# A diffusion backbone's first stage rebuilt: four latent projections per feature tile, context keys and values by group

## The chip, the core and the metric

The kernel runs on one core of one Trainium2 chip. The time is device microseconds of that core for one execution; it stands as the median of three runs. Five engines take part: TensorE (PE; its weight loads are listed as PEld), VectorE (DVE), ScalarE (ACT), GpSimd (POOL) and SyncE (SP, which issues most transfers).

## The reference

Two layers run over 1024 latent tokens of width 1024, with 256 context tokens beside them. The first is windowed attention (16 query heads in four groups, head width 128), the second a convolution module. Shift, scale and gate of each layer come from a linear map of a condition vector.

```python
shift, scale, gate = split(silu(c) @ ada_w[i] + ada_b[i], 3)        # 1024 -> 3 x 1024
h_lat = rmsnorm(x, norm_g[i]) * (1 + scale) + shift                 # latent tokens
h_ctx = the same of ctx with silu(c_ctx)                            # layer 0 only
# layer 0
q, k, v, z = h_lat @ w_in       # 2048, 512, 512, 2048 columns; q and k rotated by position
kc, vc     = h_ctx @ w_in[:, k and v columns]
o = softmax([sink, q kc, q k (|i-j| <= 128)] / sqrt(128)) @ [vc, v]
x = x + gate * ((o * silu(z)) @ w_out)
# layer 1
a, gl, z = h_lat @ w_in + b_in
u = layernorm(depthwise_conv31(a * sigmoid(gl)) + b)
x = x + gate * ((silu(u) * silu(z)) @ w_out)
return rmsnorm(x, final_g)
```

All inputs and outputs are fp32.

## The kernel before

**Arithmetic.** A matmul with full precision is done as three matmuls of type fp32r: each operand is split into a high half (a copy on ACT, L147) and a low half (a subtraction of the high half on DVE or POOL, `split_lo`, L156), and `mm3` (L194) multiplies high by high, high by low and low by high. So each operand costs an ACT copy and a DVE or POOL subtraction before PE can use it. Activations are kept turned: feature on the partition, token along the row. A *feature tile* is 128 of the 1024 features (eight tiles, `kt`), a *pair* (`pr`) two of them, a *half* 512 of the 1024 tokens.

**Places.** SBUF is handed out in 45 pages of 4 KB per partition (`pg`, names that end in `_page`) and 6 smaller ones (`hp`, `_half`). PSUM has two tiles of two banks (`ps_s`, shown as pss), two single banks o0 and o1 (`ps_o`, pso) and a pair of banks (`ps_g`, psg). Weights of the attention layer come in 512 KB chunks of 128 columns (`WStream`, L199: `load` issues the transfer on SP's queue, `split` makes the halves, `need` does both if they are late, `done` frees).

**Order.** Every engine call goes through the class `InOrder` (L77), which is why each row of the trace has line 87. A scheduler orders the instructions of an engine by its own estimate, unless `pin` (L104) puts the engine into program order. Before, nothing is pinned in the first stage, and PE alone from line 999 on.

**First stage (L303 to L463 and L987 to L998).** For each of four pairs: the modulation vector of the pair's 256 features is computed by 512-column matmuls over the condition vector (8 of plain fp32 for each of pairs 0 and 3, 16 of fp32r with split weights for each of 1 and 2; L384 to L399), its row is copied out of PSUM and turned into columns by four small matmuls (L403 to L413). Then the pair's two context tiles are modulated and split, and the keys and values of the context of all four groups are accumulated in the two pss tiles, 8 x 3 matmuls of 256 columns per tile (L421 to L436; weights from `kv_load`, L290). Then the pair's two latent tiles of the first half are modulated and split, and two projections are accumulated: keys of group 0 and queries of head 0 (`kq`, L447 to L458). Rows of the context and the first half are normalised and turned ahead of that (`normalise`, L326; `turned`, L335), those of the second half after the last pair's matmuls are issued. After the loop the second half is modulated (`mod_x1`), keys and queries are rotated (`rope`, L805, which swaps halves by two transfers on ACT's queue), context keys and values are split (`ctx_out`, L488), and three more half projections run alone (L995 to L998).

**Attention (L1000 to L1052).** 16 heads by 8 query blocks of 128 give 128 steps. A step issues the scores of the next block (`scores`, L900; the softmax behind them runs on DVE, ACT and POOL), then 12 matmuls of a later projection as fill (`fill`, L887, from the queue `fillq`: the gate z and the query of the coming heads, each 48 matmuls), then the product with the values for a half of a head (`pv`, L956), then the transposes of the block's softmax (`transposes`, L935). Where the next head opens a group (`regroup`, L1024), the group's keys and values are projected at that place. Background work runs in small pieces: `ada_rest` (the remaining modulation vectors, on DVE) and `low_parts` (low halves of the output weights).

**Then** comes the attention's output projection (`proj_attn`, L627) in four quarters of half by 512 columns, each with four blocks of 128 tokens in PSUM banks listed at L694; its first matmuls are already used as fill in the last head (`early_proj`, from block `EARLY_FROM`). In the last quarter the last three weight pieces are held back and each block is finished by itself, followed by its evacuation (`evac0`, L728). The conv stage and the kernel's output projection follow, the latter with the same scheme of quarters and a bank list of its own.

## Time and profile before

| | |
|---|---|
| median of three runs | 1807.83 us (1807.12 to 1808.11) |
| profiled execution, time and span | 1810.63 us, 1808.8 us |
| mean granted TensorE clock | 0.986 |
| busy share PE, PEld | 96%, 79% |
| busy share DVE, ACT, POOL | 69%, 49%, 45% |
| moved by DMA | 246.66 MB, mean 136 GB/s |

The share of busy time is an average over stages. Rows of the trace read: start in us, duration in us, engine, line, operation, output tile and inputs, shape and type, then in brackets how long the engine stood idle before it and what released it. Matmuls are pipelined, so their durations overlap, and PE's rate is read from the distance of their starts. A row of the view by stretches gives the stretch, its length, the busy time and count of PE, PEld, DVE, ACT and POOL in this order, the granted TensorE clock as a share of full speed, the busy share of the DMA engines and the GB/s that they moved. Tile names are the program's without their numbers: `araw`, `ahi`, `alo` are the modulation weights and their halves, `wraw`, `whi`, `wlo` the projection weights', `kvh` and `kvl` the context weights', `fc` and `fx` modulated context and latent tiles before they are split into `hch`, `hcl` and `hh`, `hl`; `x_page` holds token rows.

### The profile page before, as it was taken

To read this page: it belongs to the slowest core of one execution; us is meant where nothing else is said; L and a number is where in the kernel's file an instruction comes from. 1 tells how busy PE (TensorE), PEld (TensorE's weight loads), DVE (VectorE), ACT (ScalarE), POOL (GpSimd) and SP (SyncE) were. 2 spreads that over 40 slices of the span, in tenths; PEclk is the share of its full clock that TensorE was granted. 3 is DMA by queue.
4 is the path that set the end of the run, shared out by engine and by line. 5 is a ranking of instruction groups with operands and counts; after the bars stand their busy time and mean duration, and the time that the engine had idled before them with its cause. 6 is when DMAs were issued, how large, how long until landed. Compare 5 with 4: busy or idle time off the path is not lost. (4 is left out here: it accounts for less than half of the span.)

```text
span 1808.8 us, 23987 instructions
## 1 busy us (share of the span) xinstructions
PE 1740.4 (96%) x8383; PEld 1425.1 (79%) x8383; DVE 1253.6 (69%) x2429; ACT 883.3 (49%) x1535; POOL 812.9 (45%) x624
## 2 busy tenths in 40 slices
PE   6889999999999999999999989999999999999997
PEld 3577888888778887888788877888888888788886
DVE  5566677577657875675614349999999999866733
ACT  4444444445444554444533426655556565366630
POOL 1553334233433344342200137999888788220300
PEclk8999999999999999999999999999999999999999
DMA  9422344244334444333877723111020202376881
GB/s 339 136 63 82 114 152 143 90 136 143 117 105 128 149 135 130 91 120 120 302 279 244 261 76 104 48 35 47 24 88 30 82 30 70 113 247 227 316 290 47
DMA packets 196478, 246.66 MB, mean 136 GB/s; under 512 B 11926, under 2 KB 126918, under 8 KB 196356
## 3 DMA queue, kind: packets, MB, share of 16 engines
q1 hardware_dynamic: 189668, 234.29, 39.2%
q10 hardware_dynamic: 6688, 10.83, 2.4%
q8 instruction: 66, 1.08, 0.2%
q14 instruction: 56, 0.46, 0.1%
HBM read 192.90 MB, written 41.69 MB: 130 GB/s over the span
## 5 line engine op out<-in xcount | busy, mean ns | idle before, releaser
L87 POOL TENSOR_TENSOR odd_half<-odd_half,prod_half 128x513 f32<-128x513 f32 (+2 forms) x252 | 318.0, 1269 | 20.9 <-ACT prod_half L87 7.4
L87 PE MATMUL psg<-hh_page,whi_page 128*128 128x512 f32 x632 | 253.6, 401 | 3.1 <-DVE rope_half L87 3.1
L87 PE MATMUL psg<-hh_page,wlo_page 128*128 128x512 f32 x632 | 251.4, 398 | 0.0
L87 PE MATMUL psg<-hl_page,whi_page 128*128 128x512 f32 x632 | 251.3, 398 | 0.0
L87 POOL TENSOR_TENSOR wlo_page<-wraw_page,whi_page 128x1024 fp32r<-128x1024 f32 x72 | 174.9, 2431 | 139.8 <-ACT whi_page L87 87.6
L87 POOL TENSOR_SCALAR p_page<-p_page,sc 128x640 f32<-128x640 f32 (+1 forms) x128 | 104.8, 819 | 284.5 <-DVE sc L87 149.0
L87 ACT ACTIVATE prod_half<-ubuf,dww 128x513 f32<-128x513 f32 (+2 forms) x252 | 165.2, 674 | 110.2 <-POOL odd_half L87 106.2
L87 ACT ACTIVATE p_page<-p_page,sc 128x640 f32<-128x640 f32 (+1 forms) x128 | 102.6, 801 | 170.2 <-DVE sc L87 162.2
L87 PE MATMUL psg<-h2l_page,whi_page 128*128 128x512 f32 x456 | 179.6, 394 | 1.8 <-DVE h2l_page L87 1.8
L87 PE MATMUL psg<-h2h_page,whi_page 128*128 128x512 f32 x456 | 181.1, 397 | 0.0
L87 PE MATMUL psg<-h2h_page,wlo_page 128*128 128x512 f32 x456 | 179.7, 394 | 0.0
L87 DVE SCALAR_TENSOR_TENSOR pss<-ubuf,wsum,pss 128x512 f32<-128x512 f32 (+3 forms) x270 | 172.7, 674 | 0.3
L87 DVE SCALAR_TENSOR_TENSOR pss<-ubuf,dww,pss 128x512 f32<-128x512 f32 (+3 forms) x270 | 172.5, 674 | 0.3
L87 PEld LDWEIGHTS psg<-hh_page,wlo_page 128*128 128x128 f32 x632 | 120.1, 190 | 28.2
L87 PEld LDWEIGHTS psg<-hh_page,whi_page 128*128 128x128 f32 x632 | 120.7, 191 | 26.3 <-DVE rope_half L87 3.5
L87 PEld LDWEIGHTS psg<-hl_page,whi_page 128*128 128x128 f32 x632 | 120.5, 191 | 22.4
L87 PE MATMUL pso<-h2l_page,whi_page 128*128 128x512 f32 x312 | 122.9, 394 | 0.0
L87 PE MATMUL pso<-h2h_page,whi_page 128*128 128x512 f32 x312 | 122.9, 394 | 0.0
L87 PE MATMUL pso<-h2h_page,wlo_page 128*128 128x512 f32 x312 | 122.6, 393 | 0.0
L87 ACT ACTIVATE whi_page<-wraw_page 128x1024 fp32r<-128x1024 f32 x88 | 92.8, 1054 | 60.9 <-PE psg L87 20.4
L87 DVE TENSOR_TENSOR ptlo<-pss,pthi 128x640 fp32r<-128x640 f32 (+1 forms) x144 | 103.0, 715 | 25.9 <-ACT pthi L87 25.7
L87 ACT ACTIVATE pthi<-pss 128x640 fp32r<-128x640 f32 (+1 forms) x144 | 88.3, 613 | 65.0 <-PE pss L87 48.5
(247 smaller groups left out, 4080.9 us busy)
## 6 DMA issues: line engine op xcount, KB each, us to landing
wraw_page<-in_conv_w_in_dram SPq DMA_DIRECT2D x48, 512.0 KB, 3.9
wraw_page<-in_attn_w_in_dram SPq DMA_DIRECT2D x40, 512.0 KB, 4.7
wo_page<-in_attn_w_out_dram SPq DMA_DIRECT2D x32, 512.0 KB, 4.3
wol_page<-wolA SPq DMA_DIRECT2D x32, 512.0 KB, 7.5
wo_page<-in_conv_w_out_dram SPq DMA_DIRECT2D x32, 512.0 KB, 8.1
wol_page<-wolC SPq DMA_DIRECT2D x32, 512.0 KB, 7.0
rope_half<-rope_half ACTq DMA_DIRECT2D x80, 128.0 KB, 2.4
araw_page<-in_ada_w_dram SPq DMA_DIRECT2D x32, 256.0 KB, 4.6
```

The costliest lines, as they stand in the source:

```text
L87: r = f(*a, **k)
```

## The change

- **Loads.** The first half's latent rows come first, then three pairs of modulation weights with two weight chunks behind each of the first two, then the context rows. The separate 4 MB load of key and value weights is gone.
- **Modulation.** All but one 256-row piece is split and multiplied as fp32r. The functions `ada_split`, `ada_mm` and `ada_cols` are called a pair ahead of the tiles that use them.
- **First half.** For each feature tile, four projections of the latent tokens (key, query, value, gate of head 0) run instead of two, into the four banks of the pss tiles. Latent tiles are modulated straight out of the transposes' bank. PE and DVE are pinned to program order.
- **Context.** Context tiles are turned, modulated and split as cover between the latent ones. Keys and values of the context are projected for group 0 only, and for the other groups in their own jobs (a third part, `half == 2`); the tiles `hch` and `hcl` stay until the last group's values are done.
- **Second half.** Four projections per tile again, each tile modulated two tiles ahead; the first scores are issued after its sixth tile's matmuls. The remaining outputs are emptied in the order value, key, query, gate.
- **Attention.** 18 matmuls of the next head's query run before the loop; then the query of a coming head stands ahead of its gate in the queue. The early part of the output projection starts at the last head's first block, at 10 matmuls a step. A weight chunk is split after 15 matmuls of a job's second part instead of at the end of its first. At a change of group the gate that is left in the queue is issued first. One of the two extra steps of `ada_rest` moves from block 3 to block 1.
- **Last quarters.** The bank lists of the two last quarters alternate the pss tiles: (2, 3, 0, 1) becomes (2, 0, 3, 1) in the attention projection, (5, 0, 1, 2) becomes (0, 5, 1, 2) in the kernel's last. Banks 0 and 1 are the halves of one pss tile, 2 and 3 of the other.

```diff
+SPLIT_AT = 14
+ADA_FP = ((0, 0),)
+LAST_FILL = 10
 FILL = 12
 DEFER = 6
 EARLY = 2
 EARLY_ROWS = 6
-EARLY_FROM = 4
+EARLY_FROM = 0
...
-    add_chunk(("q", 0), wcol(0))
-    add_chunk(("v", 0), wv[0])
-    add_chunk(("k", 0), wk[0])
-    for g in range(NG):
-        for h in range(4 * g, 4 * g + 4):
-            add_chunk(("z", h), wcol(AW + 2 * KW + h * P))
-            if h + 1 < NH:
-                add_chunk(("q", h + 1), wcol((h + 1) * P))
-        if g + 1 < NG:
-            add_chunk(("k", g + 1), wk[g + 1])
-            add_chunk(("v", g + 1), wv[g + 1])
-    wsA = WStream(chunks, lo_eng=lambda i: V if i in (1, 2) else G)
+    for key, src in (("k", 0), wk[0]), (("q", 0), wcol(0)), (("v", 0), wv[0]), (("z", 0), wcol(AW + 2 * KW)):
+        add_chunk(key, src)
+    for h in range(NH - 1):
+        add_chunk(("q", h + 1), wcol((h + 1) * P))
+        add_chunk(("z", h + 1), wcol(AW + 2 * KW + (h + 1) * P))
+        if h % 4 == 3:
+            add_chunk(("k", h // 4 + 1), wk[h // 4 + 1])
+            add_chunk(("v", h // 4 + 1), wv[h // 4 + 1])
+    wsA = WStream(chunks, nraw=4, lo_eng=lambda i: V if i in (2, 4) else G)
...
-    def kv_load(pr):
-        kvraw[pr] = [pg.alloc(F32, [1024], "kvraw") for _ in range(2)]
-        for i in range(2):
-            kt = 2 * pr + i
-            SY.dma_start(out=kvraw[pr][i], in_=W[kt * P:kt * P + P, AW:AW + 2 * KW])
...
+    xs0 = load_rows(x[0, 0:512], 4)
     ada_load(0)
+    wsA.load()
+    wsA.load()
+    ada_load(1)
+    wsA.load()
+    wsA.load()
+    ada_load(2)
     cx = load_rows(ctx[0], 2)
-    kv_load(0)
-    xs0 = load_rows(x[0, 0:512], 4)
-    wsA.load()
...
-    ck = [ps_s(), ps_s()]
-    kq = None
-    wq = None
-    def mod_x1(kt):
-        h, l = Hh[kt][:, 512:1024], Hl[kt][:, 512:1024]
-        modulate(fx1[kt], fx1[kt], kt, 0)
-        act(h, fx1[kt], AF.Copy)
-        split_lo(G if kt % 2 else V, l, fx1[kt], h)
-        if kt % 2:
-            pg.free(fx1_pg[kt // 2])
-    for pr in range(NPR):
...
-            for j in range(8):
-                c = ck[j // 4][:, j % 4 * CT:j % 4 * CT + CT]
-                mm3(c, wh[:, j], wl[:, j], h, l, kt == 0 and j % 2 == 0, kt == KT - 1 and j % 2 == 1)
...
-            mm3(kq[0], wh[:, 0], wl[:, 0], h, l, kt == 0, kt == KT - 1)
-            mm3(kq[1], wq[0][:, kt], wq[1][:, kt], h, l, kt == 0, kt == KT - 1)
...
+    def ada_split(pr):
+        for i in range(4):
+            if (pr, i) not in ADA_FP:
+                raw = araw[pr][i]
+                rv = raw.rearrange("p a b c -> p a (b c)")
+                h, l = pg.alloc(F32R, [2, 512], "ahi"), pg.alloc(F32R, [2, 512], "alo")
+                act(h, rv, AF.Copy)
+                split_lo(V, l, rv, h)
+                pg.free(raw)
+                araw[pr][i] = (h, l)
+    def ada_mm(pr):
+        o = ps_o(0)
+        for i in range(4):
+            for k in range(2):
+                if (pr, i) in ADA_FP:
+                    r = araw[pr][i].rearrange("p a b c -> p a (b c)")
+                    parts = [(cf, r)]
+                else:
+                    parts = [(c4, r) for r in araw[pr][i]]
+                for n, (c, r) in enumerate(parts):
+                    PE.matmul(o[0:4], c[:, 2 * i + k, :], r[:, k], start=i + k + n == 0,
+                              stop=i + k == 4 and n == len(parts) - 1)
+            pg.free(*(araw[pr][i] if len(parts) == 2 else (araw[pr][i],)))
+        V.tensor_copy(R[pr][0:4, 0:512], o[0:4])
+    def ada_cols(pr):
+        rw, m = R.pop(pr), mods[pr]
+        cps = ps_o(1)
+        for i in range(4):
+            PE.matmul(cps[:, 2 * i:2 * i + 2], rw[0:5, i * P:(i + 1) * P], sel[0:5], start=True, stop=True)
+        hp.free(rw)
+        with tc.high_priority():
+            V.tensor_copy(m[:, 0:2], cps[:, 0:4].rearrange("p (a b) -> p a b", b=2))
+            for i in range(2):
+                V.tensor_scalar(out=m[:, 2 + i], in0=cps[:, 4 + 2 * i:6 + 2 * i], scalar1=1.0,
+                                scalar2=vt[:, 96 + 2 * pr + i:97 + 2 * pr + i], op0=ALU.add, op1=ALU.mult)
+    def turn(ts, kt, bank):
+        tp = bank()
+        for i in range(len(ts)):
+            PE.transpose(tp[:, i * P:(i + 1) * P], ts[i][:, kt * P:(kt + 1) * P], ident)
+        return tp
+    def x_tile(tp, kt, half, eng):
+        if half == 0:
+            Hh.append(pg.alloc(F32R, [1024], "hh"))
+            Hl.append(pg.alloc(F32R, [1024], "hl"))
+        sl = slice(half * 512, half * 512 + 512)
+        m, i = mods[kt // 2], kt % 2
+        with tc.high_priority():
+            modulated(tp, [(Hh[kt][:, sl], Hl[kt][:, sl], lambda f: f[:, 0:512])], m[:, 2 + i, 0:1], m[:, i, 0:1], 512, eng)
+    def c_tile(kt, bank=1):
+        m, i = mods[kt // 2], kt % 2
+        if kt % 4 == 0:
+            Hc.append((pg.alloc(F32R, [4, CT], "hch"), pg.alloc(F32R, [4, CT], "hcl")))
+        h, l = (t[:, kt % 4] for t in Hc[kt // 4])
+        modulated(turn(cx, kt, lambda: ps_o(bank))[:, 0:CT], [(h, l, lambda f: f[:, 0:CT])],
+                  m[:, 2 + i, 1:2], m[:, i, 1:2], CT, V)
+        if kt == KT - 1:
+            pg.free(*cx)
+    def x_mm(kt, half, acc, which):
+        sl = slice(half * 512, half * 512 + 512)
+        for n in which:
+            w = wsA.hl[n]
+            mm3(acc[n], w[0][:, kt], w[1][:, kt], Hh[kt][:, sl], Hl[kt][:, sl], kt == 0, kt == KT - 1)
...
+    pin("PV")
+    normalise(xs0, (V, V, G, G))
+    ada_split(0)
+    ada_mm(0)
+    ada_load(3)
+    ada_cols(0)
+    for _ in range(2):
+        wsA.split()
+    tps = [turn(xs0, kt, ps_g) for kt in range(2)]
+    sa, sb = ps_s(), ps_s()
+    acc0 = [t[:, i * 512:i * 512 + 512] for t in (sa, sb) for i in range(2)]
+    ctodo = deque(range(KT))
+    x_tile(tps[0], 0, 0, V)
+    x_tile(tps[1], 1, 0, V)
+    x_mm(0, 0, acc0, (0, 1))
+    x_mm(1, 0, acc0, (0, 1))
+    ada_split(1)
+    for _ in range(2):
+        wsA.split()
+    for pr in range(NPR):
+        a, b = 2 * pr, 2 * pr + 1
+        which = range(4) if pr else (2, 3)
+        if pr + 1 < NPR:
+            ada_mm(pr + 1)
+        if pr == 1:
+            normalise(cx, (G, G))
+        if pr == NPR - 1:
+            normalise(xs1, (G, G, G, G))
+        if pr + 2 < NPR:
+            ada_split(pr + 2)
+        x_mm(a, 0, acc0, which)
+        if pr + 1 < NPR:
+            tp = turn(xs0, a + 2, ps_g)
+            ada_cols(pr + 1)
+            x_tile(tp, a + 2, 0, V)
+        if pr > 1:
+            c_tile(ctodo.popleft())
+        x_mm(b, 0, acc0, which)
+        if pr + 1 < NPR:
+            x_tile(turn(xs0, b + 2, ps_g), b + 2, 0, G)
+        if pr > 0:
+            c_tile(ctodo.popleft())
+        if pr == 1:
+            xs1 = load_rows(x[0, 512:1024], 4)
...
-            acc = [banks[b] for b in ((4, 5, 0, 1), (2, 3, 4, 5), (0, 1, 4, 5), (2, 3, 0, 1))[s]]
+            acc = [banks[b] for b in ((4, 5, 0, 1), (2, 3, 4, 5), (0, 1, 4, 5), (2, 0, 3, 1))[s]]
...
+        if kind in "kv" and half == 2:
+            c = kvt[n][2]
+            if kind == "k":
+                act(c[:, 0], o[:, 0:CT], AF.Copy)
+                split_lo(V, c[:, 1], o[:, 0:CT], c[:, 0])
+                return None
...
+    def gemm_ctx(wc, o):
+        for kt in range(KT):
+            h, l = (t[:, kt % 4] for t in Hc[kt // 4])
+            for a, b in ((0, h), (0, l), (1, h)):
+                PE.matmul(o[:, 0:CT], wc[a][:, kt], b, start=kt == 0 and a == 0 and b is h, stop=kt == KT - 1 and a == 1)
+                yield
+    PARTS = {"q": (0, 1), "z": (0, 1), "k": (0, 1, 2), "v": (2, 0, 1)}
...
+            for m, _ in enumerate(gh):
+                yield
+                if m == DEFER - 1 and late:
+                    late()
+                if m == SPLIT_AT and half == PARTS[kind][1] and wsA.ns <= i + 1:
+                    wsA.split()
+                    wsA.load()
...
-            kc = (kch, kcl)[b]
             PE.matmul(s[:, w0:512], q[a][:, qsl], kk[b][:, ksl], start=n == 0, stop=n == 2)
-            PE.matmul(s[:, 512:768], q[a][:, qsl], kc[:, g], start=n == 0, stop=n == 2)
+            PE.matmul(s[:, 512:768], q[a][:, qsl], c[:, b], start=n == 0, stop=n == 2)
...
+    pin("P")
+    tps = []
+    while ctodo:
+        c_tile(ctodo.popleft(), len(ctodo) % 2)
+        if len(tps) < 2:
+            tps.append(turn(xs1, len(tps), ps_g))
+    d0 = [target(kind, 0) for kind in "kqvz"]
+    tails = []
+    def finished0(half, acc, which=range(4)):
+        for n in which:
+            t = finish("kqvz"[n], 0, half, acc[n], d0[n])
+            if t:
+                tails.append(t)
+    finished0(0, acc0)
+    for kind, n in (("k", 0), ("v", 2)):
+        o = ps_g()
+        for _ in gemm_ctx(wsA.hl[n], o):
+            pass
+        t = finish(kind, 0, 2, o, d0[n])
+        if t:
+            tails.append(t)
+        x_tile(tps.pop(0), n // 2, 1, V)
...
+    sa = ps_s()
+    acc1 = [sa[:, 0:512], sa[:, 512:1024], ps_g(), ps_g()]
     for kt in range(KT):
-        mod_x1(kt)
-    rope(kq[0], h0, *(t[:, h0] for t in kvt[0]))
-    rope(kq[1], h0, *(t[:, h0] for t in qt[0]))
-    ctx_out()
-    run(job(("v", 0), (0,)))
+        x_mm(kt, 1, acc1, range(4))
+        if kt + 2 < KT:
+            x_tile(turn(xs1, kt + 2, lambda: ps_o(kt % 2)), kt + 2, 1, G if kt % 2 else V)
+        if kt >= 2 and tails:
+            tails.pop(0)()
+        if kt == 0:
+            wsA.load()
+        if kt == 5:
+            pg.free(*xs1)
+            wsA.split()
+            scores(0, 0)
+    for i in range(4):
+        wsA.done(i)
+    wsA.nraw = 2
+    wsA.load()
+    finished0(1, acc1, (2, 0, 1, 3))
...
-    run(job(("k", 0), (1,)))
-    run(job(("q", 0), (1,)))
-    pin("P")
...
-    scores(0, 0)
     pvq = deque()
-    enqueue(("z", 0))
     enqueue(("q", 1))
-    run(job(("v", 0), (1,)))
+    fill(18)
+    tails.pop()()
     for _ in range(2):
         next(adag)
     for i, (h, qb) in enumerate(steps):
         if qb == 0:
             if h + 1 < NH:
+                if h:
+                    enqueue(("q", h + 1))
                 enqueue(("z", h + 1))
-            if h + 2 < NH:
-                enqueue(("q", h + 2))
...
-        if lstate[0] == "open" or h and (h % 4 < 3 or qb < LOWS):
+        if lstate[0] == "open" or 0 < h < NH - 1 and (h % 4 < 3 or qb < LOWS):
...
-            fill(FILL)
+            fill(FILL if h < NH - 1 else LAST_FILL)
...
+            fill(1000, ("z", h + 1))
             run(job(("k", g)))
...
-        for _ in range(2 if qb == 3 or qb == 6 and h % 2 else 1):
+        for _ in range(2 if qb == 1 or qb == 6 and h % 2 else 1):
...
-            acc = [banks[b] for b in ((0, 1, 2, 3), (4, 5, 0, 1), (2, 3, 6, 4), (5, 0, 1, 2))[s]]
+            acc = [banks[b] for b in ((0, 1, 2, 3), (4, 5, 0, 1), (2, 3, 6, 4), (0, 5, 1, 2))[s]]
```

More of the change, by code (lines that the diff above doesn't have):

```diff
@@ L823, in job @@
         wc = wsA.need(i)
[L824 to L839 removed]
+        d = target(kind, n)
```

234 lines of the change are left out of this document (54 added, 180 removed).

## The prediction

> **What bounds the kernel now.** I read the page first, then the busy time in stretches of 20 us, then PE's waits in order of time, then the other engines' instructions around those waits.
>
> ```profile
> PE 1740.4 (96%) x8383; PEld 1425.1 (79%) x8383; DVE 1253.6 (69%) x2429; ACT 883.3 (49%) x1535; POOL 812.9 (45%) x624
> ```
> ```profile
> 0.00:20.00 20.00, 10.26 (x25) 2.50 (x25) 3.40 (x15) 7.31 (x11) 1.63 (x8) 1.00 0.83 292
> 20.00:40.00 20.00, 14.73 (x76) 11.14 (x76) 17.07 (x28) 10.73 (x20) 6.10 (x3) 0.70 1.08 374
> 40.00:60.00 20.00, 14.84 (x71) 8.81 (x69) 14.90 (x21) 10.98 (x16) 10.43 (x5) 0.84 0.89 301
> 60.00:80.00 20.00, 20.00 (x98) 11.41 (x97) 8.07 (x17) 9.19 (x16) 5.91 (x3) 0.95 0.34 106
> 80.00:100.00 20.00, 18.09 (x121) 16.03 (x121) 13.01 (x25) 8.94 (x14) 13.98 (x9) 0.91 0.07 24
> 100.00:120.00 20.00, 16.84 (x80) 13.61 (x79) 14.27 (x17) 10.02 (x17) 11.62 (x8) 0.91 0.30 79
> 120.00:140.00 20.00, 18.45 (x94) 15.00 (x93) 8.03 (x22) 8.07 (x15) 6.46 (x5) 1.00 0.22 56
> ```
> PE is busy 1740.4 of 1808.8 us, so no edit that keeps the matmuls can win more than the 68 us of idle time, plus what PE loses while its clock is low. The first 140 us hold 26.8 of those 68 us (140 less the seven PE columns) and nearly all of the low clock (0.70 to 0.95 in five of seven rows). That is the stage that is rebuilt. After it PE runs dry only in short waits, which come below.
>
> **The yardstick.** The scores of the second query block, the same step in both programs, compare the two first stages.
>
> ```profile
> 60.08 0.63 PE L87 MATMUL pso<-ahi_page,c 128*4 128x512 f32 x1
> 60.50 0.63 PE L87 MATMUL pso<-alo_page,c 128*4 128x512 f32 x1
> ...
> 64.06 0.28 PE L87 MATMUL pss<-hcl_page,kvh_page 128*128 128x256 f32 x1
> 64.18 0.28 PE L87 MATMUL pss<-hch_page,kvl_page 128*128 128x256 f32 x1
> ...
> 84.92 0.40 PE L87 MATMUL psg<-hh_page,kvh_page 128*128 128x512 f32 x1
> 85.16 0.39 PE L87 MATMUL psg<-hl_page,kvh_page 128*128 128x512 f32 x1
> ...
> 100.83 0.60 PE L87 MATMUL pso<-ident,x_page 128*128 128x128 f32 x4
> ...
> 137.17 0.42 PE L87 MATMUL pss<-kh_page,qh_page 128*128 128x384 f32 x1
> ```
> Matmuls overlap, so their price is the distance between starts: about 0.23 us for 512 columns (0.42 while the clock is low), 0.12 for 256. Before, the second scores start at 137.17. By then PE has done 144 big matmuls (keys, queries and values of group and head 0), all 192 context matmuls and all modulation. After, the instruction order puts 210 big ones ahead of these scores (four projections of 48, and 18 of the next query) and 48 context ones. What still follows differs: before, the gate of head 0 and 48 of the next query, 96 x 0.23 = 22.2 us; after, 144 context matmuls and 30 of the query, 144 x 0.12 + 30 x 0.23 = 24.0 us. So a first stage whose second scores start at T gains 137.2 - (T + 1.8).
>
> **The first stage after, step by step.** VectorE and PE now keep the written order there, so I walk along VectorE.
>
> ```profile
> 18.45 0.67 DVE L87 COPY arow_half<-pso 4x512 f32<-4x512 f32 x1
> ...
> 24.10 0.34 DVE L87 TENSOR_SCALAR mod<-pso,vt 128x2 f32<-128x2 f32 x2
> ...
> 35.40 1.22 DVE L87 TENSOR_TENSOR alo_page<-araw_page,ahi_page 128x1024 fp32r<-128x1024 f32 x1
> 36.54 2.73 DVE L87 TENSOR_SCALAR x_page<-x_page,r 128x1024 f32<-128x1024 f32 x4
> ...
> 53.30 1.80 DVE L87 TENSOR_TENSOR alo_page<-araw_page,ahi_page 128x1024 fp32r<-128x1024 f32 x1
> 55.02 2.43 DVE L87 TENSOR_SCALAR fc_page<-fc_page,mod 128x256 f32<-128x256 f32 x1
> ...
> 75.66 0.42 DVE L87 TENSOR_TENSOR hcl_page<-fc_page,hch_page 128x256 fp32r<-128x256 f32 x1
> 76.55 0.69 DVE L87 TENSOR_TENSOR hl_page<-fx_page,hh_page 128x512 fp32r<-128x512 f32 x1 [0.47 <-ACT hh_page L87]
> ```
> ```profile
> 32.55 2.42 POOL L87 TENSOR_TENSOR alo_page<-araw_page,ahi_page 128x1024 fp32r<-128x1024 f32 x1
> 53.98 3.33 POOL L87 TENSOR_TENSOR alo_page<-araw_page,ahi_page 128x1024 fp32r<-128x1024 f32 x1
> 77.42 1.30 POOL L87 TENSOR_TENSOR hl_page<-fx_page,hh_page 128x512 fp32r<-128x512 f32 x1 [4.64 <-ACT hh_page L87]
> 82.15 4.43 POOL L87 TENSOR_SCALAR x_page<-x_page,r 128x1024 f32<-128x1024 f32 x4 [3.43 <-issue]
> ```
> ```profile
> 15.28 1.06 ACT L87 ACTIVATE junk_page<-x_page 128x1024 f32<-128x1024 f32 x1 [0.19 <-DMA x_page<-in_ctx_dram]
> 16.45 1.28 ACT L87 ACT_TABLE_LOAD   x1
> ...
> 30.09 3.90 ACT L87 ACTIVATE ahi_page<-araw_page 128x1024 fp32r<-128x1024 f32 x4
> ```
> - Loads. The context rows, 3 MB deep in the queue, were there at 15.1 us. The latent rows now go first, 2 MB: about 11 us (9 to 15). Through the fourth modulation pair the queue holds 13 MB; before, 0.292 x 20 + 0.374 x 20 = 13.3 MB had moved by 40 us, so its pages land at about 39, when VectorE first wants them (44, below). The 4 MB of key and value rows are gone.
> - Start. Four squares on ACT behind the last page (12), table 1.3, root and six small steps 1.5, rows normalised on two engines 2.2 (POOL's 2 of 4.43/4): 17. Three low halves of pair 0 at 1.2, each after ACT's 1.0: 20.5. Then the last modulation matmuls, row copy 0.7, turning it, 0.5 for the scalars, modulation 0.7, ACT 0.6: the first tile multiplies at 25 (23 to 28).
> - Pair 1 and 2. From 27 VectorE's order reads: four low halves 4.9, one weight half 1.2, row copy 0.7, four low halves 4.9, scalars 0.5, modulation 0.7. A POOL weight half falls between: the 1.80 us low half began at 53.30, inside POOL's stretch, and took 0.6 longer than the 1.22 one; I count POOL's 2.4 in full. Together 15.3: the third tile starts at 42.5. PE's own work from 25 to there is 56 matmuls, 13 us at 0.23 and 24 at 0.42: close behind VectorE where it is cold, waiting for it where it is warm.
> - Pair 3. Low half, modulation, row copy, 2.1; the context's root 1.0 behind a 1.3 POOL tile half; four low halves 4.9; POOL's two context rows 2.2; scalars and modulation 1.2: tile 4 at 55. With that the splits are spent. Tiles 4 to 7 then cost PE 2.8 each plus 0.7 for turns, and one more round of scalars at 61: all eight done at 70.
> - Between the halves. Three context tiles (0.4 + 0.4 + 0.4 each), two latent tiles, and a rotary add in VectorE's order that waits for its swap: the last context low half at 79, 24 context matmuls behind it 2.9: second half from 82.
> - Second half: 96 x 0.23 + 6 turns x 0.6 + 1.7 for scores and small turns = 27.5: 109.5. Emptying the value bank before the next query's matmuls 1.5, 18 matmuls 4.2, a turn 0.6: T = 116.
>
> Gain 137.2 - 117.8 = **20 us**. Low end: PE never waits after 25; 144 more matmuls and the rest are then some 78 us, T = 103, gain 32. High end: T = 128, gain 7 (a rival below). I keep 116, because VectorE's list alone fills 27 to 55.
>
> **The other terms.**
>
> ```profile
> 177.62 0.38 PE L87 MATMUL pss<-kh_page,ql_page 128*128 128x256 f32 x1 [2.97 <-POOL ql_page L87]
> ...
> 478.45 0.63 PE L87 MATMUL pss<-kh_page,qh_page 128*128 128x384 f32 x1 [1.86 <-DVE ptlo L87]
> ...
> 502.97 1.33 PE L87 MATMUL pss<-ident,p_page 128*128 128x128 f32 x5 [2.61 <-POOL p_page L87]
> ...
> 1055.78 0.50 PE L87 MATMUL pss<-woh_page,ozh_page 128*128 128x512 f32 x1 [0.84 <-DVE x_page L87]
> 1068.53 0.50 PE L87 MATMUL pss<-woh_page,ozh_page 128*128 128x512 f32 x1 [4.08 <-DVE rq L87]
> ...
> 1790.59 0.50 PE L87 MATMUL pss<-woh_page,gs_page 128*128 128x512 f32 x1 [0.78 <-DVE x_page L87]
> ```
> - Query ahead of gate in each head's fill: the rotated query is ready four steps sooner, so 2.97 goes, with some five matmuls 0.19 slower behind it: -4 (-2 to -6).
> - Last quarter of the attention projection. Block 2 and 3 now write a half of a PSUM tile whose other half was emptied one block (4.2 us) earlier. The 0.84 goes. Block 3 waits for block 1's evacuation instead of block 2's, and the new order on VectorE has that evacuation ahead of the row-scale chain that held it to 1064.5 before. So the 4.08 goes too, and with it the low clock: of 18 matmuls some 8 started 0.42 apart, 1.6. Sum -6.5 (-2 to -6.5). VectorE's chain for block 3 moves forward with PE; it was last before, and is next late, but PE has the next stage's matmuls.
> - Last quarter of the kernel: -0.8, the same wait; the chain after the last block is unchanged.
> - Head 0's fill. The gate of head 0 is done already, so 78 fill matmuls stand for 8 steps of 12: one and a half steps have none. Their price is a wait for the softmax, 2.61 at its longest above, and a third of that for the half step: +3.5 (0 to 7, with a cold start).
> - Last head. The early projection's 72 matmuls are spread over 8 steps of 10 and end with the head; two softmax ends are uncovered, 1.86 by the nearest row, and the second has half of the cover: +2.8 (0 to 5).
> - Group changes: context keys and values bring 48 matmuls to each of three changes, moved, not added, and the gate before them is flushed as cover: 0 (-4 to +4).
> - Conv stage: the order on PE, VectorE and POOL is the same, 0.
>
> Sum: -20 - 4 - 6.5 - 0.8 + 3.5 + 2.8 = -25. The profiled execution spans 1808.8 and took 1810.6; the median is 1807.8, the frame of my number: **1783**.
>
> **The rivals.**
> 1. POOL stops VectorE throughout. POOL has some 20 us of work up to the second half (three weight halves 7.2, eight rows 8.9, three tile halves 3.9), and I charged 5.9 of it to VectorE's list. At 55.02 a quarter-size modulation took 2.43 until POOL's low half ended; if every POOL instruction did so, T = 128 to 130: about 1796. Against it: ScalarE and the loads leave VectorE pauses in which POOL can run. The Trainium skill (SBUF — State Buffer, "SBUF: two separate sides") calls the port that the two share an exclusive lock held for a whole instruction; the two rows agree. By that rule alone the time is this rival's.
> 2. PE paces the stage. If the splits run ahead, as ACT and VectorE were only 55% and 85% busy from 20 to 40 us, T = 103: about 1770. Against: the order has pair 2's splits ahead of pair 1's scalars.
> 3. Slower than before. In the second half each tile must be modulated two tiles ahead. Before, the same chain made PE wait here, and the clock fell:
> ```profile
> 92.84 0.80 PE L87 MATMUL psg<-hh_page,kvh_page 128*128 128x512 f32 x1 [1.84 <-ACT hh_page L87]
> ```
> If each of eight tiles waits 1.84 and starts cold (12 x 0.19), that is 4.1 x 8 = 33 us: 1816. From 3.1 us a tile on it eats the gain. For it: POOL's 1.3 per odd tile. Against: the chain is 0.7 + 0.6 + 0.7 (1.3), under two tiles' 5.6.
> 4. It does nothing: the idle time only moves into the attention steps, whose fill is thinner by 18. That would need waits of some 23 us in two heads; the longest row is 2.61. It would end near 1806.
>
> **How the numbers follow.** My forecast has 0.56 (its own range 1775 to 1791), rival 1 0.20, rival 2 0.12, rival 3 0.08, rival 4 0.04. Eight in ten: 1768, where rival 2 ends with the lower bounds of the small terms, to 1802, rival 1 with the upper ones. A measurement of this kernel tells 0.2% (3.6 us) from no change: faster 0.87, within 0.04, slower 0.09.
>
> **What would show it.** The second scores near 116 us, PE busy two thirds of 20 to 60 at a low clock, VectorE with low halves back to back there, PE full in the second half; no wait for a rotated query at a head's start; no 4 us wait at the attention projection's end; short waits for the softmax at the ends of heads 0 and 15. Wrong if the second scores come after 130, or if the attention steps wait in many heads.

## The result and the profile after

The changed kernel took 1833.3 us (median of four, 1828.6 to 1836.3) beside 1807.97 us before: ratio 1.0136, 95% interval 1.0113 to 1.016. It is 25 us slower, where 25 us faster was forecast. Its profiled execution took 1828.6 us (span 1826.8) and is the fastest of its four, while the one of before (1810.6) lies above its median. So the two traces differ by 18.0 us, and what makes the other 7 us between the medians no trace shows.

First the page of the profile after, its row of busy time for PE:

```profile
PE 1736.8 (95%) x8383; PEld 1425.5 (78%) x8383; DVE 1234.2 (68%) x2424; ACT 880.0 (48%) x1526; POOL 814.3 (45%) x618
```

PE, VectorE and ScalarE all have a little less to do than before; the 18 us are idle time of PE (90.0 us instead of 68.4). Where PE waits between 100 and 1100 us, before and then after (what was waited for: us in total, times, longest):

```profile
PE pss L87 <- POOL p_page L87: 6.6, 6, 2.6
PE pss L87 <- POOL ql_page L87: 4.8, 4, 3.0
PE pss L87 <- DVE rq L87: 4.1, 1, 4.1
PE pss L87 <- DVE sc L87: 4.0, 5, 1.0
...
PE pso L87 <- DVE ptlo L87: 1.0, 2, 0.7
```
```profile
PE pss L90 <- POOL p_page L90: 30.1, 17, 3.0
PE pss L90 <- DVE sc L90: 6.0, 8, 1.5
PE pso L90 <- DVE ptlo L90: 5.2, 6, 1.3
...
PE pss L90 <- DVE ptlo L90: 3.5, 3, 2.8
```

The waits that the forecast wanted gone are gone (`ql_page`, `rq`). In their place PE waits 30.1 us for the normalised softmax block (`p_page`), 17 times.

The first stage and the borders of the heads, in PE's rows of before and after:

```profile
900.69 0.40 PE L87 MATMUL pss<-woh_page,ozh_page 128*128 128x512 f32 x1
...
1074.38 0.39 PE L87 MATMUL psg<-h2h_page,whi_page 128*128 128x512 f32 x1
```
```profile
28.61 0.79 PE L90 MATMUL pss<-hh_page,whi_page 128*128 128x512 f32 x1 [0.71 <-ACT hh_page L90]
...
47.84 0.40 PE L90 MATMUL pss<-hh_page,whi_page 128*128 128x512 f32 x1
...
61.13 0.39 PE L90 MATMUL pss<-hh_page,whi_page 128*128 128x512 f32 x1
...
90.05 0.39 PE L90 MATMUL pss<-hh_page,whi_page 128*128 128x512 f32 x1
...
122.78 0.42 PE L90 MATMUL pss<-kh_page,qh_page 128*128 128x384 f32 x1
...
926.10 0.39 PE L90 MATMUL pss<-woh_page,ozh_page 128*128 128x512 f32 x1
...
1092.45 0.40 PE L90 MATMUL psg<-h2h_page,whi_page 128*128 128x512 f32 x1
```

The second scores come at 122.78 instead of 137.17, so the first stage gained 14.4, less 1.8 of moved matmuls: 12.6 us. The output projection of the attention lasts 166.35 instead of 173.69 us: 7.3 gained. Between them the heads take 803.3 instead of 763.5 us: 39.8 lost, of which only the 1.8 was accounted for. This is the whole loss.

To see where in a head it sits, I take from the trace the start of each block's scores on PE and sum, over heads 1 to 14, the distance from one block's scores to the next block's (the first interval runs from block 0's scores to block 1's; the three changes of group are counted apart). A step opens with the scores of the next block, so a head's third step, counted from one, lies in its fourth interval, and its fifth step in the sixth. The fifth interval, for instance, holds the fill of the fourth step and the transposes of block 3; the second and sixth hold the products with the values. The rows below "after" belong to experiments that follow.

| us, heads 1 to 14 | 1 | 2 | 3 | 4 | 5 | 6 | 7 | 8 | changes |
|---|---|---|---|---|---|---|---|---|---|
| before | 53.7 | 97.1 | 59.4 | 61.2 | 69.3 | 112.9 | 61.2 | 56.8 | 101.2 |
| after | 47.4 | 102.6 | 59.6 | 59.8 | 91.0 | 120.0 | 65.0 | 48.2 | 123.1 |
| gate first | 36.0 | 114.8 | 60.0 | 59.9 | 61.3 | 111.9 | 61.1 | 106.7 | 131.8 |
| soft order | 47.4 | 107.0 | 58.9 | 60.9 | 61.2 | 122.2 | 69.9 | 51.0 | 123.2 |
| halves | 50.7 | 115.0 | 67.1 | 59.9 | 62.9 | 112.3 | 61.2 | 45.4 | 136.4 |
| gate lead of 18 | 59.6 | 115.3 | 60.6 | 59.9 | 67.0 | 110.1 | 62.8 | 51.1 | 130.1 |
| gate lead of 24 | 77.9 | 111.6 | 58.9 | 59.6 | 62.9 | 111.6 | 61.2 | 52.5 | 108.2 |
| order, weights, late step | 51.7 | 102.0 | 58.9 | 59.4 | 65.0 | 114.0 | 64.4 | 59.2 | 118.2 |

The fifth to seventh intervals grew by 32.6 us, the second by 5.5. Of the 30.1 us of waits for the normalised block, 21.7 fall into the fifth intervals. The changes and the eighth together grew by 13.3, less than the 17.3 of context matmuls (144 x 0.12) that moved there.

One fifth interval (head 6) in the trace after. PE, then VectorE, then GpSimd:

```profile
425.04 0.42 PE L90 MATMUL pss<-kh_page,qh_page 128*128 128x384 f32 x1
...
436.35 0.77 PE L90 MATMUL pss<-ident,p_page 128*128 128x128 f32 x5 [2.99 <-POOL p_page L90]
```
```profile
427.83 0.81 DVE L90 CUSTOM_DVE_ANT_0 p_page<-pss,mask_page 128x640 f32<-128x640 f32 x1
...
430.42 1.53 DVE L90 SCALAR_TENSOR_TENSOR mask_page<-dww_raw,cs,mask_page 128x256 f32<-128x256 f32 x1
431.87 0.68 DVE L90 TENSOR_TENSOR rope_half<-rope_half,rope_half 128x512 f32<-128x512 f32 x1
432.47 0.14 DVE L90 TENSOR_TENSOR sc<-sc 128x1 f32<-128x1 f32 x1
432.54 0.81 DVE L90 CUSTOM_DVE_ANT_0 p_page<-pss,mask_page 128x640 f32<-128x640 f32 x1
...
434.77 0.15 DVE L90 RECIPROCAL sc<-sc 128x1 f32<-128x1 f32 x1
```
```profile
430.20 1.47 POOL L90 TENSOR_TENSOR rope_half<-rope_half,sin_page 128x512 f32<-128x512 f32 x1 [2.12 <-DMA rope_half<-rope_half]
433.30 1.27 POOL L90 TENSOR_TENSOR ql_page<-rope_half,qh_page 128x512 fp32r<-128x512 f32 x1 [1.63 <-ACT qh_page L90]
435.02 1.28 POOL L90 TENSOR_SCALAR p_page<-p_page,sc 128x640 f32<-128x640 f32 x1 [0.46 <-DVE sc L90]
```

Block 3's scores are issued at 425.04 and reduced at 427.83. GpSimd then takes up the rotation of the next query's first half, which waits 2.12 us for its swap transfer. VectorE has the rotation's sum (431.87) ahead of the softmax's own small steps (432.47 and, behind block 4's reduction, 434.77). The normalisation starts at 435.02, ten microseconds behind the scores, and PE has stood still for 2.99. The rotation is here because the query now comes first in each head: its first half is complete after two steps of fill.

### The profile page after: what moved, and what is told of

Its sections match the earlier page's. It is cut to its first block, busy times and chain, and to the rows that moved or that the text cites. A ratio compares the mean times of both kernels' runs of the same rounds, so it can differ in the third digit from the quotient of the medians.

```text
span 1826.8 us, 23984 instructions
## 1 busy us (share of the span) xinstructions
PE 1736.8 (95%) x8383; PEld 1425.5 (78%) x8383; DVE 1234.2 (68%) x2424; ACT 880.0 (48%) x1526; POOL 814.3 (45%) x618
## 5 line engine op out<-in xcount | busy, mean ns | idle before, releaser
L90 POOL TENSOR_SCALAR p_page<-p_page,sc 128x640 f32<-128x640 f32 (+1 forms) x128 | 116.1, 907 | 319.0 <-DVE sc L90 185.7
L90 PE MATMUL psg<-hh_page,whi_page 128*128 128x512 f32 x592 | 236.1, 399 | 1.2 <-DVE kvc_page L90 0.7
L90 PE MATMUL psg<-hh_page,wlo_page 128*128 128x512 f32 x592 | 234.7, 396 | 0.0
L90 PE MATMUL psg<-hl_page,whi_page 128*128 128x512 f32 x592 | 234.4, 396 | 0.0
L90 ACT ACTIVATE prod_half<-ubuf,dww 128x513 f32<-128x513 f32 (+2 forms) x252 | 164.9, 674 | 110.1 <-POOL odd_half L90 106.2
L90 PEld LDWEIGHTS psg<-hh_page,wlo_page 128*128 128x128 f32 x592 | 112.1, 189 | 26.2
L90 PEld LDWEIGHTS psg<-hh_page,whi_page 128*128 128x128 f32 x592 | 112.8, 190 | 22.1 <-DVE kvc_page L90 1.2
L90 PEld LDWEIGHTS psg<-hl_page,whi_page 128*128 128x128 f32 x592 | 112.8, 190 | 20.7
L90 PE MATMUL pss<-ident,p_page 128*128 128x128 f32 x608 | 89.5, 277 | 38.6 <-POOL p_page L90 30.1
L90 PE MATMUL pso<-h2h_page,whi_page 128*128 128x512 f32 x312 | 122.8, 394 | 0.0
L90 PE MATMUL pso<-h2h_page,wlo_page 128*128 128x512 f32 x312 | 122.8, 394 | 0.0
L90 PEld LDWEIGHTS pss<-ident,p_page 128*128 128x128 f32 x608 | 71.3, 141 | 59.9 <-POOL p_page L90 46.3
```

The source lines that it names most:

```text
L90: r = f(*a, **k)
```

## The experiments

Each stands beside the kernel before on the same chip, which took 1806.3 to 1807.5 us on all of them; so the changed kernel's 1833.3 is the comparison where none is named.

**GpSimd wholly in program order.**

```diff
+    pin("PG")
     steps = [(h, qb) for h in range(NH) for qb in range(TB)]
```

> The changed kernel with GpSimd, too, kept in program order through the attention heads; nothing else. Theory A (in the changed kernel the rotary product of the next query, which waits for its swap transfer, stands ahead of a softmax block's normalisation on GpSimd; 30.1 us of PE waits on p_page against 6.6 before): the order is turned round, the waits on p_page fall below 10 us and the time by 15 to 25, to some 1808 to 1818 us. Theory B (the cover is simply too thin, since fill matmuls moved to the first stage and the groups' contexts): the waits stay within 5 us of 30 and the time within 4 of 1833.

Measured: 1942.6 us. PE's waits of that run:

```profile
PE psg L90 <- POOL wlo_page L90: 113.8, 30, 8.3
PE pss L90 <- POOL p_page L90: 10.2, 7, 3.2
```

The waits on the softmax fell to 10.2 and the fifth intervals to 61.2 us, as theory A wants, and 113.8 us of waits for weight halves came up, which it had not foreseen: the halves now stand behind the next normalisation, nine matmuls before they are used.

**The same, weights split earlier** (`SPLIT_AT = 0`).

> GpSimd in program order through the heads, as in the first run, and the weight chunk split at the first matmul of a job's second part, two steps ahead of its use instead of nine matmuls. Theory A' (the order on GpSimd costs the fifth to seventh blocks their 32 us, and the 113.8 us of waits for wlo_page in the first run only come from the split standing behind the next normalisation with nine matmuls to go): both waits fall below 12 us, the fifth block stays at 4.2 to 4.5 us a head, 1795 to 1812 us. If program order on GpSimd is harmful by itself (the weight halves are late at any place): above 1833, with waits for wlo_page over 30 us.

Measured: 1892.8 us, waits on `p_page` 4.6 us, on `wlo_page` still 81.5. So strict order is harmful by itself: a weight half may wait for nothing, but stands behind the rotation, which does. In head 6 the rotation's low half, at 420.64, had waited 3.63 us for ScalarE, and the weight half came behind it at 421.86.

**The split alone** (`SPLIT_AT = 0`, nothing else).

> The changed kernel with the weight chunk split at the first matmul of a job's second part instead of the fifteenth. If GpSimd's 2.5 us weight halves are what delays the softmax's normalisation: 10 us or more faster or slower, with the waits on p_page moved. Theory A (the rotary product is it): within 5 us of 1833, p_page waits 25 to 35 us.

Measured: 1837.5 us, `p_page` waits 34.8. The place of the split is not the cause.

**Gate before query** (the main lines; the weight chunks and the flush at a change of group follow the same order).

```diff
-                if h:
-                    enqueue(("q", h + 1))
                 enqueue(("z", h + 1))
+                if h:
+                    enqueue(("q", h + 1))
```

> The changed kernel with the gate of a coming head ahead of its query in the fill queue again, from head 1 on (weight chunks in the same order). Theory A (the query's rotation, now in the middle of a head, is what stands in the softmax's way): the long interval of the fifth block of each head (7.2 us against 4.2 to 5.2 before) goes back to 4.2 to 5.5, waits for a rotated query of 0.5 to 3 us come back at head starts; together 10 to 20 us faster, 1813 to 1823. Theory B (thin cover): no change beyond 4 us.

Measured: 1854.8 us. Row "gate first" of the table: the fifth interval is cured (61.3), but the eighth doubles. PE waits:

```profile
PE pss L90 <- ACT qh_page L90: 27.8, 9, 4.3
PE pss L90 <- POOL p_page L90: 7.9, 8, 1.8
```

The query is now complete only when the next head begins. Where the rotation goes, the wait goes; the total was missed, since nothing keeps the queue ahead here.

**Fill of 11 and 13.**

```diff
+FILLS = (11, 11, 11, 11, 13, 13, 13, 13)
-            fill(FILL if h < NH - 1 else LAST_FILL)
+            fill(FILLS[qb] if h < NH - 1 else LAST_FILL)
```

> The changed kernel with 11 fill matmuls in each of a head's first four steps and 13 in the last four, so that a query's second half ends four matmuls into the fifth step, the long one with the product with the values, instead of at the end of the fourth. Theory A (what costs is that the rotation's work on ScalarE, VectorE and GpSimd falls on a short step): the fifth interval falls from 6.5 us on average to below 5, with nothing in its place: 12 to 25 us faster, 1808 to 1821. Theory B (thin cover): the fifth interval gets longer as its fill shrinks, 1833 or more.

Measured: 1838.9 us, fifth intervals 98.5. The second half's rotation was moved to the fifth step and nothing got better: theory A had the wrong half. Theory B's forecast came true in both numbers (waits on `p_page` 43.4 us); that thin cover alone is not the cause is seen only in the next run, where the fill stays as it is. What costs is the rotation of the first half, which begins with the third step in both kernels and meets block 3's softmax there, as the rows of head 6 show. That is theory A2.

**The softmax ahead of the rotation, and nothing else ordered.** `GP` is a second handle on GpSimd in program order, used for the normalisation and for the rotation's product and low half.

```diff
-        tt(G, w, w, sin[:, sl], ALU.mult)
+        tt(GP, w, w, sin[:, sl], ALU.mult)
...
-        split_lo(G, dl, r, dh)
+        split_lo(GP, dl, r, dh)
...
-        G.tensor_scalar(out=p[:, 0:w], in0=p[:, 0:w], scalar1=ri, scalar2=1.0, op0=ALU.mult, op1=ALU.mult)
+        GP.tensor_scalar(out=p[:, 0:w], in0=p[:, 0:w], scalar1=ri, scalar2=1.0, op0=ALU.mult, op1=ALU.mult)
```

> The changed kernel; of GpSimd's work only the softmax's normalisation and the two instructions of each rotation are kept in program order, the weight halves are left to the scheduler. Theory A2 (the rotation of a query's first half, which begins with a head's third step, stands ahead of block 3's softmax on GpSimd and, by the sum behind it, on VectorE): the normalisation goes first, the fifth interval falls from 6.5 us on average to below 4.8, waits on p_page below 12 us, waits for wlo_page stay below 10: 1800 to 1815 us. If VectorE's load in that step is the cause and not the order: fifth interval and time as before, 1828 to 1838.

Measured: 1817.0 us (1816.5 to 1821.0), 16 us faster, fifth intervals 4.4 us each. PE and GpSimd at the same place of head 6 (block 3's scores; the normalisations of blocks 2 and 3), and the wait that was 30.1:

```profile
427.79 0.42 PE L90 MATMUL pss<-kh_page,qh_page 128*128 128x384 f32 x1
```
```profile
431.19 0.80 POOL L90 TENSOR_SCALAR p_page<-p_page,sc 128x640 f32<-128x640 f32 x1 [4.83 <-ACT rope_half L90]
436.15 0.81 POOL L90 TENSOR_SCALAR p_page<-p_page,sc 128x640 f32<-128x640 f32 x1 [4.15 <-DVE sc L90]
436.92 1.46 POOL L90 TENSOR_TENSOR rope_half<-rope_half,sin_page 128x512 f32<-128x512 f32 x1
```
```profile
PE pss L90 <- POOL p_page L90: 12.7, 10, 2.9
```

The rotation follows block 3's normalisation, which starts 8.4 us behind the scores instead of 10.0. One change of order is worth 16 of the 25 us in this kernel: this part of the cause is shown. What it does not cure are the second, sixth and seventh intervals (107.0, 122.2, 69.9).

**Projections by halves** (gate, query, gate, query, 24 matmuls each, so that both rotations begin with a step that has a product), alone and with the order above. The main lines:

```diff
-                if h:
-                    enqueue(("q", h + 1))
-                enqueue(("z", h + 1))
+                for half in (0, 1):
+                    enqueue(("z", h + 1), (half,))
+                    if h:
+                        enqueue(("q", h + 1), (half,))
```

> The changed kernel with the two coming projections taken by halves in turn (gate, query, gate, query, 24 matmuls each), so that both rotations begin with a step that has a product with the values (the first and fifth of a head). Theory A2: no softmax is due while they run; the fifth interval falls below 4.8 us and no wait takes its place: 1800 to 1815. If only the order on GpSimd matters and not the step: the normalisation is again behind a rotation, the waits on p_page stay above 20 us.

> Both edits of the two kernels before it. Theory A2: as good as the better of the two, 1798 to 1812, waits on p_page below 10 us. If the two edits cure the same thing, no more than 4 us below the better of them.

Measured: 1834.6 and 1843.2 us. Alone, the fifth intervals went to 62.9 and the sixth to 112.3, but the second and third and the changes took it back (row "halves"). Theory A2's price for both was wrong. With the order the kernel is even 8.6 us slower, and waits on `p_page` are 21.1 instead of 14.7 us: the order pays where the rotation meets block 3's softmax, not everywhere.

**The queue ahead by part of a gate**, so that the rotations begin in the fifth and seventh steps, as they mostly did before; with the order; and with 24 instead of 18.

```diff
+                enqueue(("q", h + 1) if h else ("z", 1))
+                if h % 4 < 3 and h + 2 < NH:
+                    enqueue(("z", h + 2))
...
             scores(*nxt)
+            enqueue(("z", h + 2))
+            fill(18)
```

> The changed kernel with 18 matmuls of a coming gate always ahead in the queue: 18 matmuls are also issued at each change of group, and from head 1 on the queue holds the rest of the coming gate, the coming query, then 18 of the next gate. So a query's first rotation begins six matmuls into a head's fifth step (the long one) and its second six into the seventh, as in the heads before the change, where the queue also ran ahead. Theory A3 (what the change lost in the heads is this phase, and nothing else of it): the fifth interval falls below 5 us, the first to eighth intervals are together within 8 us of those before, 1784 to 1800 us, faster than before. If the thinner head 0, the contexts in the changes of group or the scheduler's order are what costs: 1812 to 1835.

> The same with the softmax's normalisation and the rotations in program order on GpSimd, as in the soft order run. Theory A3: within 6 us of the run without it, since no softmax waits behind a rotation. If the order on GpSimd still costs there: 8 us or more faster than it.

> As the first of these three with a lead of 24 matmuls instead of 18, so that the rotations begin with the first fill matmul of the fifth and seventh steps; head 0 and a step at each change of group lose 6 and 12 fill matmuls. Theory A3: the same within 5 us. If the start within the step decides (next to the scores' softmax or six matmuls after it): more than 8 us apart.

Measured: 1830.1, 1827.6 and 1819.7 us. With a lead of 18 the fifth to seventh intervals are those of before (67.0, 110.1, 62.8), and yet the sum is no better: the first two and the changes are longer. So theory A3 falls; the step in which the rotations begin is not the whole cause. The place within the step is not that of before, though: in head 6 ScalarE's first copy for the rotation starts 2.6 us into the sixth interval, in the kernel before 7.0 us into it. And that place counts: the lead of 24, which theory A3 puts within 5 us of the lead of 18, is 10.4 us faster, and with GpSimd's order left alone it is 13.6 us faster than the changed kernel. Its changes of group are short and its first intervals long (108.2 and 77.9); why was not separated, and it was not run together with the order. The order is worth 2.5 us at a lead of 18. One second interval, of 14.87 us, in head 10 of the first of these, VectorE and then GpSimd:

```profile
629.68 1.43 DVE L90 SCALAR_TENSOR_TENSOR mask_page<-wsum_raw,cs,mask_page 128x256 f32<-128x256 f32 x1 [2.48 <-DMA wsum_raw<-in_ada_w_dram]
631.03 2.82 DVE L90 TENSOR_TENSOR rope_half<-rope_half,rope_half 128x512 f32<-128x512 f32 x1
```
```profile
630.79 2.52 POOL L90 TENSOR_TENSOR wlo_page<-wraw_page,whi_page 128x1024 fp32r<-128x1024 f32 x1
634.90 0.69 POOL L90 TENSOR_SCALAR p_page<-p_page,sc 128x512 f32<-128x512 f32 x1 [1.60 <-ACT qh_page L90]
```

VectorE waits 2.48 us for a transfer of the background modulation, and then needs 2.82 us for a sum that takes 0.68 alone, while GpSimd makes a weight half; the softmax stands behind both.

**Background work.** The extra step of the modulation back at its old place (`qb == 3`); the weight halves on VectorE (`G if i in (0, 1, 3) else V`); this with the order; all three together.

> The changed kernel with the extra step of the background modulation after a head's fourth block again instead of its second, so that VectorE has one instruction less (0.5 to 1.5 us) between the scores of block 3 and its normalisation. If VectorE's load in that step is the cause: the fifth interval falls by 0.5 us or more a head, 7 to 15 us faster. Theory A2: within 4 us of 1833.

> The changed kernel with the low halves of the attention weights, from the fifth chunk on, on VectorE (1.2 us each) instead of GpSimd (2.5 us each). Theory D (in the last runs a GpSimd weight half stretched a VectorE instruction from 0.7 to 2.8 us in front of the softmax: what is left of the loss is VectorE held up by GpSimd): the weight halves' stretch goes, 6 to 15 us faster, 1818 to 1827, the fifth interval still long. If VectorE is simply too full: it gets 1.2 us more to do 32 times, 1833 to 1845.

> The same with the softmax and the rotations in program order on GpSimd (the soft order run gave 1817). Theory D: the sixth and seventh intervals, 17 us longer than before there, lose most of it, as does the second; 1800 to 1810 us. If VectorE is too full: 1817 or more.

> The same with the extra step of the background modulation after the fourth block again (4.7 us faster by itself). If the three causes add up: 3 to 6 us below the run without it, at best 1796. If the softmax's order has already taken that away: within 2 us of it.

Measured: 1828.6, 1830.2, 1811.8 (1802.6 to 1815.1) and 1806.8 us (1802.9 to 1810.0), the last as fast as before (0.9995, 0.9984 to 1.0007). Alone, neither of the first two can be told apart from the changed kernel by more than its scatter of 8 us, and the late step left the fifth intervals at 90.4, so that instruction is not what made them long. Behind the order, each takes 5 us more off. With the weight halves on VectorE the second, sixth and seventh intervals fall by 6.6, 5.7 and 6.3 us from those of the soft order run, as theory D wants (100.4, 116.5, 63.6), while the eighth grows by 8.5. The waits on `p_page` are 26.2 us again in the last run, but 2.5 of them in the fifth intervals and 11.6 in the eighth: the wait has moved once more, and what stands beside it has shrunk.

**The last head as before** (`EARLY_FROM = 4`, `LAST_FILL = 12`, low halves into the last head).

> The changed kernel with the early output projection from the last head's fifth block at 12 matmuls a step, and the low halves of the output weights spread into the last head, as before. Theory C (heads 14 and 15 took 7.7 and some 6 us longer than the moved work explains, because what was left of the low halves is run at once at the start of the last head): 8 to 13 us faster, 1820 to 1825. If the early projection itself is not the cause: within 4 us of 1833.

Measured: 1842.0 us, 9 slower. Head 14 became short (41.4 instead of 48.7 us), but the last head took 67.8 instead of 48.9. Theory C falls: taken together, these three edits were a gain.

**The first stage without GpSimd** (its rows, weight halves and tile halves of the first half on VectorE).

> The changed kernel with everything that GpSimd does in the first half of the first stage (two latent rows, two context rows, three weight halves, three tile halves; 24 us of its time) put on VectorE instead. If GpSimd's instructions stop VectorE's for as long as they share operands' memory (rival 1 of the prediction), VectorE's list grows by 9 us of own work and loses about as much of stretched work: the second scores stay within 3 us of 122.8. If GpSimd's help is real, they come 6 us or more later.

Measured: 1836.0 us, second scores at 124.49 instead of 122.78. VectorE's low halves of pair 1, here and in the changed kernel, where GpSimd makes a weight half in the same stretch:

```profile
33.24 4.62 DVE L90 TENSOR_TENSOR alo_page<-araw_page,ahi_page 128x1024 fp32r<-128x1024 f32 x4
```
```profile
31.61 6.83 DVE L90 TENSOR_TENSOR alo_page<-araw_page,ahi_page 128x1024 fp32r<-128x1024 f32 x4
```

They take 1.15 instead of 1.71 us each. Some 24 us of GpSimd's work were worth 1.7 us. The Trainium skill (SBUF — State Buffer, "SBUF: two separate sides") has a VectorE instruction with two SBUF inputs and a GpSimd instruction that reads SBUF exclude each other for a whole instruction; these rows agree (the four took 2.2 us longer beside a weight half of GpSimd).

**The kernel before with the two bank lists alone.**

```diff
-            acc = [banks[b] for b in ((4, 5, 0, 1), (2, 3, 4, 5), (0, 1, 4, 5), (2, 3, 0, 1))[s]]
+            acc = [banks[b] for b in ((4, 5, 0, 1), (2, 3, 4, 5), (0, 1, 4, 5), (2, 0, 3, 1))[s]]
...
-            acc = [banks[b] for b in ((0, 1, 2, 3), (4, 5, 0, 1), (2, 3, 6, 4), (5, 0, 1, 2))[s]]
+            acc = [banks[b] for b in ((0, 1, 2, 3), (4, 5, 0, 1), (2, 3, 6, 4), (0, 5, 1, 2))[s]]
```

> The kernel before with the two bank lists of the last quarters changed and nothing else. The prediction's terms: the waits of 0.84 and 4.08 us at the attention projection's end and 0.78 us in the last quarter go, 1.6 us of low clock with them: 5 to 8 us faster, 1799 to 1803. If the wait moves to the next stage instead: within 2 us of before.

Measured: 1799.9 us, ratio 0.996 (0.9945 to 0.9975), projection 166.6 us. The two lines are worth 7.5 us beside 1807.4 on the same chip, and this kernel is the fastest of all.

## Why the prediction was wrong

- **First stage, gain 20.** Right in kind, 12.6 in size. The first tile multiplied at 28.6 (25 forecast), the third at 47.8 (42.5), tile 4 at 61.1 (55), the second half began at 90.1 (82) and took its 27 us as worked out. The mis-sized term at the start is the low half at 1.2 us: the three of pair 0 took 6.53 us beside GpSimd's weight halves and 3.49 without them (all fifteen 23.4 us, 1.6 on average), which is most of the first 3.6 us. Rival 1 had this mechanism, but the second scores at 122.8 lie between its 128 and the forecast's 116. From the first tile to the third PE waited only 0.5 us in 19.2, so there its own list set the pace too (rival 2's mechanism, without its time): 19.2 us where 17.5 were forecast.
- **A slip in the yardstick.** 96 x 0.23 is 22.1 and 144 x 0.12 + 30 x 0.23 is 24.2, so 2.1 us moved, not 1.8. The 0.3 us change nothing.
- **Query ahead of gate, -4.** The step that failed. The term counted the wait at a head's start that goes. That part came: the first intervals fell by 6.3 us, 2.8 of it because 12 fill matmuls fewer lie in them, and the other 3.5 are close to the 4. It put at nothing the place where the moved rotation's own instructions fall: two transfers and two instructions each on VectorE, ScalarE and GpSimd per half, now in the third to fifth steps, where they meet block 3's softmax. The fifth to seventh intervals grew by 32.6 us, nine times the 3.5. Of this the fifth's 21.7 are shown to be the rotation's: every run that moves or reorders it brings them back to 61.2 to 67.1, except the fill of 11 and 13, which moved the other half. The order on GpSimd alone is worth 16 us of the kernel's time.
- **The extra step of the background modulation**, moved from block 3 to block 1, has no term in the forecast. Put back, it is worth 4.7 us alone, within the scatter, and 5.0 behind the order and the weights.
- **Rival 4** (idle time moves into the heads) was right in direction. Its bound was wrong: it weighed the 2.61 us of one wait against two thinly filled heads, but waits of 1.5 to 3.0 us came in the fifth interval of nine heads of the fourteen. This is the second of the prediction's own signs of being wrong. Rival 3's second-half chain did not appear.
- **Attention projection, -6.5, and last quarter, -0.8.** Right: -7.3 and the 0.78 wait gone; -7.5 together on the chip.
- **Head 0, +3.5, last head, +2.8, group changes 0.** By the same account of starts, less the moved matmuls (18 fewer in head 0, 36 fewer in the last head, the contexts in the changes): +5.0, +3.4 and -4.0 (with the eighth interval). Small misses, together 1.9 us in the change's favour.

What stays open: the three edits together win back the 26.6 us, but the first stage and the quarters had gained nearly 20, so even there the heads take 778.8 us where 765.3 were due. Which of the remaining meetings of softmax, rotation and background make these 13.5 us was not separated, nor why a lead of 24 matmuls does so much better than one of 18.

## What to carry to other kernels

When a piece of work moves in a queue, price every instruction that hangs on it at the place where it lands, on each engine that runs in order: an instruction that waits for a transfer holds up all that stands behind it. A softmax that takes some 8 us from scores to normalisation (427.79 to 436.15 in the soft order run), in steps of 4.2 us, leaves little room wherever the work is put: of the other places tried here, the best gained 13.6 us. Ordering only the urgent chain gained 16, ordering the whole engine lost 109. GpSimd's help is worth little where VectorE's instructions get longer beside it.

## What was not expected of the hardware

A VectorE sum of 0.68 us took 2.82 beside a 2.52 us instruction of GpSimd, and low halves 1.71 instead of 1.15. Moving 24 us of GpSimd's work onto a busy VectorE delayed the stage by 1.7 us only.
